# Requesting the last modulation section's weight chunks one at a time into two slots

## The chip, the cores and the metric

The kernel runs on one core of a Trainium2 chip. The metric is the device time of one execution in microseconds, as a median over runs. The core has a matrix engine (PE, with PEld for its weight loads), a vector engine (DVE), a scalar engine (ACT), a general engine (POOL), and SP, which only issues transfers. Each engine takes its own instructions strictly in the order in which they are written; engines wait for each other through semaphores. Transfers (DMA) are carried out by 16 DMA engines, fed here by two main queues: SP's requests (q1) and POOL's requests (q0).

## The reference

One conditioned decoder block on a sequence of 512 positions and a width of 1024. What matters here:

```python
mod = jax.nn.silu(c) @ w_ada + b_ada
shift1, scale1, gate1, shift2, scale2, gate2 = [m[:, None, :] for m in jnp.split(mod, 6, axis=-1)]
...
h2 = rms_norm(x, norm2_g) * (1.0 + scale2) + shift2
f_g, f_u = jnp.split(h2 @ w_ffn_in, 2, axis=-1)
x = x + gate2 * ((jax.nn.silu(f_g) * f_u) @ w_ffn_out)
```

`w_ada` is 1024 x 6144, so each of the six sections of `mod` is a vector of 1024 made from a 1024 x 1024 block of weights (4 MB). The last section, `gate2`, is needed only after the second matrix product of the feed-forward part. The first product of that part has `w_ffn_in`, 1024 x 5632 (2 x 2816 columns).

## The kernel before

**The work around the change.** After the two branches, their merge and the second norm, the kernel computes `h2 @ w_ffn_in` column group by column group, and then the last product with `w_ffn_out`. The order of all instructions is written out by hand; nothing reorders them. Every product is done as three products of rounded parts (`mm3`, lines 52 to 55), with a high part made by ACT and a low part made by DVE for each block of weights. The first pair of column groups is done in plain form; the other 20 groups are done in the loop `for q in range(-2, NQ)` (here "turn q", with NQ = 18), in which a seven-product scheme replaces eight products of half blocks. An even q handles 256 columns of the gate part `f_g` (followed by silu), an odd q the same columns of `f_u` (followed by the product with the gate part). One turn holds seven calls of `sprod`, each of twelve matmuls of 128 x 256, on four PSUM banks R[0] to R[3]; even and odd turns have different banks.

**What a turn does beside the matmuls.**

- `s_issue(q + 2)`, first thing in the turn (line 1311): SP requests the weight block of the turn after next, as two halves of 512 KB. The first half holds the blocks A11 and A21, the second A12 and A22. The buffers are a ring of three and one single buffer, so that a half can be requested when the same half of the block two turns earlier has been used up. Its last readers are DVE's L1361 (first half) and L1368 (second half), which run in turn q - 1.
- `s_prep(q + 1)` prepares the block of the next turn in four steps. ACT rounds: L1337 (A11, first half only), L1348, L1358, L1365. DVE forms sums and low parts: L1340 (A21 + A22, so both halves), L1343, L1344, L1351, L1354, L1361, L1368.
- ACT copies one bank into the next as its starting value: R[0] into R[1] (L1676), then R[1] into R[2] (L1689); two copies into `ps` (L1684, L1696). ACT's first rounding of the turn (L1337) stands ahead of the copy L1676 in its order.
- DVE adds the banks up into the result (L1701, L1704); ACT applies silu in the turns of `f_g` (L1666, L1672), DVE the product in the turns of `f_u` (L1664, L1670).
- `wstep()` (lines 1688 and 1716) lets POOL issue transfers that add up parts of `w_ffn_out` in memory, for the last product. They use POOL's queue and share the 16 engines with SP's.

**The last section.** `mod_sec(5)` yields eight chunks. A chunk is 512 KB: two slices of 128 x 512 of `w_ada`. Each has a function that requests it (line 205, on SP) and a function that uses it: two instructions of DVE on 128 x 512, here called macs, that multiply a slice by a scalar per partition and add it to `acc` (L177, or L175 for the first of each half). Chunks 0 to 3 make the first half of the section, 4 to 7 the second. `last_mod(k)` is called at the end of turns 1 to 8, with k = q - 1, after the last sums of the turn. For an even k it makes a new tile of 128 x 2 x 1024 with one buffer (tag E6), requests the chunks k and k + 1 into its two halves, and then issues the macs of chunk k; for an odd k it only issues the macs of chunk k. A new tile under the tag can be written only when the macs of the tile before have read it. In turn 9 `last_gate` uses the same buffer for the rounded result, and in turn 10 two pairs of matmuls spread it over the partitions and add it to `gate2b`.

Of the kernel before, what the change touches and what calls it, by code (L numbers as in the profile page):

```python
# [28 lines left out]
def block_kernel(ctx: ExitStack, tc: tile.TileContext, x, positions, w_ada, b_ada, w_in,  # L29
# [12 lines left out]
    def bank(k, name="bank"):  # L42
        return psum.tile([128, 512], F32, name=name, tag=f"b{k}", bufs=1)
# [28 lines left out]
    def issue(i):  # L72
        e = stream[i]
        if e["kind"] == "m" and e["early"]:
            k = mrot[0]
            mrot[0] += 1
            raw = s2pair(k % 8, F32).rearrange("p a n -> p (a n)")
        elif e["kind"] == "m" and e["mid"]:
            raw = mid.tile([128, 1024], F32, name="mraw", tag=e["mid"], bufs=1)
        else:  # L80
            raw = base.tile([128, 1024], F32, name="raw", tag="raw", bufs=RAWB)
        e["raw"] = raw
        if e["kind"] == "m":
            e["dma"](raw)
            return
        k0, nk, n = e["kts"][0], len(e["kts"]), e["n"]
        src = e["src"][k0 * 128:(k0 + nk) * 128, :]
        e["view"] = lambda t: t[:, :nk * n].rearrange("p (j n) -> p j n", j=nk)
        v = e["view"](raw)
        o = 0  # L90
        for c0, cn in (e["c0"] if isinstance(e["c0"], tuple) else ((e["c0"], n),)):
            SY.dma_start(v[:, :, o:o + cn], src[:, c0:c0 + cn].rearrange("(j p) n -> p j n", p=128))
            o += cn
# [256 lines left out]
    def t512(name, dt=F32):  # L350
        return base.tile([128, 512], dt, name=name, tag="t512", bufs=3)
# [946 lines left out]
    def s_issue(q):  # L1298
        if q >= NQ:
            return  # L1300
        c0 = (2 + q // 2) * 256 + (DFF if q % 2 else 0)
        sraw[q] = []
        both = ffn[0].tile([128, 2, 4, 2, 128], F32, name="raw", tag="E2", bufs=1) if q == -2 else None
        for kh in range(2):
            if both is not None:
                t = both[:, kh]
            elif q % 2 and kh:
                t = ffn[0].tile([128, 4, 2, 128], F32, name="raw", tag="F0" if q > 0 else "E5", bufs=1)
            else:
                t = base.tile([128, 4, 2, 128], F32, name="raw", tag="raw", bufs=RAWB)  # L1310
            SY.dma_start(t.rearrange("p j a n -> p j (a n)"),
                         w_ffn_in[kh * 512:(kh + 1) * 512, c0:c0 + 256].rearrange("(j p) n -> p j n", p=128))
            sraw[q].append(t)
# [10 lines left out]
    def s_prep(q):  # L1324

        if q >= NQ:
            return z_first()
        ra, rb = sraw[q]
        d = sd[q] = {}
        A11, A21, A12, A22 = ra[:, :, 0], ra[:, :, 1], rb[:, :, 0], rb[:, :, 1]  # L1330

        def a0():
            if q == -1:
                saw.append(sw(1, F32R, "sa"))
            d["A"] = tuple(base.tile([128, 4, 128], F32R, name="sa", tag="acc", bufs=2) if q == -2 else
                           saw[0][:, 2 * (q % 2) + e].rearrange("p (j n) -> p j n", j=4) for e in range(2))
            A.activation(d["A"][0], A11, AF.Copy)  # L1337

        def d0a():
            V.tensor_add(A21, A21, A22)  # L1340

        def d0b():
            V.tensor_sub(d["A"][1], A11, f(d["A"][0]))  # L1343
            V.tensor_sub(A11, A21, A11)  # L1344

        def a1():
            d["B"] = s_pair(q, 0)
            A.activation(d["B"][0], rb, AF.Copy)  # L1348

        def d1a():  # L1350
            V.tensor_sub(d["B"][1], rb, f(d["B"][0]))  # L1351

        def d1b():
            V.tensor_sub(rb, rb, A11[:, :, None, :].to_broadcast([128, 4, 2, 128]))  # L1354

        def a2():
            d["C"] = s_pair(q, 1)
            A.activation(d["C"][0], ra, AF.Copy)  # L1358

        def d2():  # L1360
            V.tensor_sub(d["C"][1], ra, f(d["C"][0]))  # L1361

        def a3():
            d["D"] = s_pair(q, 2)
            A.activation(d["D"][0], rb, AF.Copy)  # L1365

        def d3():
            V.tensor_sub(d["D"][1], rb, f(d["D"][0]))  # L1368
        return [(a0, d0a, d0b), (a1, d1a, d1b), (a2, d2), (a3, d3)]
# [119 lines left out]
    def gtile(m):  # L1489
        if m not in gq:  # L1490
            n = 4 if m < 20 else 2
            t = (sw((2, 3, 0)[m // 4], F32, "gq") if m < 12 else
                 ffn[0].tile([128, n, S], F32, name="gq", tag=("E5", "E6", "F1")[(m - 12) // 4], bufs=1))
            for e in range(n):
                gq[m + e] = t[:, e]
            gz[m // 4] = t
        return gq[m]
# [34 lines left out]
    mgl = list(mg)  # L1532
    mgr = []

    def last_mod(k):
        if k % 2 == 0:
            t = ffn[0].tile([128, 2, 1024], F32, name="mraw", tag="E6", bufs=1)
            mgr[:] = [t[:, 0], t[:, 1]]
            for e in range(2):
                mgl[k + e][0](mgr[e])  # L1540
        mgl[k][1](mgr[k % 2])

    def last_gate():
        t = ffn[0].tile([128, 4, S], F32R, name="ahl", tag="E6", bufs=1)
# [91 lines left out]
    def sprod(o, wb, hb, start):  # L1636
        (wh, wl), (bh, bl) = wb, hb
        for j in range(4):
            mm3(o, (wh[:, j], wl[:, j]), (bh[:, j], bl[:, j]), start and j == 0, j == 3, skip_group_check=True)

    left = []
    for q in range(-2, NQ):
        g, u = 2 + q // 2, q % 2
        d = sd[q]
        s_issue(q + 2)
        pre = s_prep(q + 1)
        half_of = lambda t, e: tuple(v[:, :, e] for v in t)
        S2_, S1_, A12, A22, S4_, S3_ = (half_of(d[k], e) for k in "CBD" for e in range(2))
        R = [bank(k, "R")[:, :256] for k in ((4, 1, 0, 7), (5, 2, 3, 6))[q % 2]]
        ps = [ffn[0].tile([128, 256], F32, name="ps", tag="rt", bufs=2) for _ in range(2)]  # L1650
        if q == NQ - 2:
            for i in W_Z[0, 0][:2]:
                issue(i)
        t0, t1 = slice(0, 256), slice(256, 512)
        if u:
            dst = [gtile(2 * g + m) for m in range(2)]
        else:
            fs[0], fs[1] = t512("fs"), t512("fs")
            dst = fs
        cur = dict(fs)  # L1660

        def out_direct(m, p, u=u, dst=dict(enumerate([dst[0], dst[1]])), cur=cur):
            if u:
                V.tensor_mul(dst[m][:, t0], cur[m][:, t0], p)  # L1664
            else:
                A.activation(dst[m][:, t0], p, AF.Silu)  # L1666

        def out_late(m, u=u, dst=dict(enumerate([dst[0], dst[1]])), cur=cur):
            if u:
                V.tensor_mul(dst[m][:, t1], dst[m][:, t1], cur[m][:, t1])  # L1670
            else:
                A.activation(dst[m][:, t1], dst[m][:, t1], AF.Silu)  # L1672

        pre[0][0]()
        sprod(R[0], d["A"], HB[0, 0], True)
        A.activation(R[1], R[0], AF.Copy)  # L1676
        for fn in pre[0][1:]:
            fn()
        while left:
            left.pop(0)()  # L1680
        if q == NQ - 1:
            issue(W_Z[0, 0][2])
        sprod(R[3], S1_, TB[1], True)
        A.activation(ps[0], R[3], AF.Copy)  # L1684
        for fn in pre[1]:
            fn()
        sprod(R[1], S2_, TB[2], False)
        wstep()
        A.activation(R[2], R[1], AF.Copy)  # L1689
        pre[2][0]()  # L1690
        pre[2][1]()
        sprod(R[0], A12, HB[1, 0], False)
        if not u:
            out_direct(0, R[0])
        sprod(R[2], S3_, TB[3], False)
        A.activation(ps[1], R[2], AF.Copy)  # L1696
        pre[3][0]()
        pre[3][1]()
        if u:
            out_direct(0, R[0])  # L1700
        V.tensor_add(dst[1][:, t1], R[3], ps[1])  # L1701
        sprod(R[1], S4_, HB[1, 1], False)
        out_late(1)
        V.tensor_add(dst[0][:, t1], R[1], ps[0])  # L1704
        sprod(R[2], A22, TB[4], False)
        out_late(0)
        left.append(lambda fn=out_direct, p=R[2]: fn(1, p))
        if 1 <= q <= 8:
            last_mod(q - 1)
        if q == 9:  # L1710
            last_gate()
        if q == 10:
            for b_ in (3, 2):
                mbank[0] = b_
                sec_tasks(one=True)
        wstep()
        if q in (9, 13, NQ - 2):
            a_sum("S1", {9: 0, 13: 2}.get(q, 1))
# [208 lines left out]
```

## Time and profile before

| | us |
|---|---|
| median of 3 runs | 822.0 (821.88 to 822.13) |
| the profiled execution | 823.29 |
| its span | 821.5 |
| PE busy | 805.9 (98%) |
| DVE busy | 686.6 (84%) |
| ACT busy | 430.9 (52%) |
| POOL busy | 166.6 (20%) |

Times of single rows count from the start of the span. "Busy" of PE counts matmuls whose ends are modelled, and they overlap. In a row of the timeline the first number is the start and the second the duration; "idle before" in square brackets names what ended the engine's wait. In the view of waits a row gives who waited, for whom, the total, how often, and the longest. In the view of transfers the last number is the time from a request to its landing. In rows of stretches the granted clock of PE, the share of DMA time and GB/s stand at the end.

### The profile page before, as it was taken

To read this page: it belongs to the slowest core of one execution; us is meant where nothing else is said; L and a number is where in the kernel's file an instruction comes from. 1 tells how busy PE (TensorE), PEld (TensorE's weight loads), DVE (VectorE), ACT (ScalarE), POOL (GpSimd) and SP (SyncE) were. 2 spreads that over 40 slices of the span, in tenths; PEclk is the share of its full clock that TensorE was granted. 3 is DMA by queue.
4 is the path that set the end of the run, shared out by engine and by line. 5 is a ranking of instruction groups with operands and counts; after the bars stand their busy time and mean duration, and the time that the engine had idled before them with its cause. 6 is when DMAs were issued, how large, how long until landed. Compare 5 with 4: busy or idle time off the path is not lost.

```text
span 821.5 us, 12945 instructions
## 1 busy us (share of the span) xinstructions
PE 805.9 (98%) x4903; PEld 719.6 (88%) x4903; DVE 686.6 (84%) x1175; ACT 430.9 (52%) x772; POOL 166.6 (20%) x186
## 2 busy tenths in 40 slices
PE   7999999999999999999999999999999999999996
PEld 6789889988888888988888899999999999888875
DVE  7989798898899648888697879889999888898686
ACT  6674445322332226665635587555555655666554
POOL 3060031363344411000010010323121322000001
PEclk9999999999999999999999999999999999999999
DMA  9974352332346563037692603989997977556763
GB/s 294 301 222 111 111 180 78 104 102 79 106 150 198 166 200 102 28 104 247 195 254 48 205 27 103 227 236 250 255 280 196 247 182 207 172 190 201 219 175 134
DMA packets 108463, 141.35 MB, mean 172 GB/s; under 512 B 6689, under 2 KB 77089, under 8 KB 108209
## 3 DMA queue, kind: packets, MB, share of 16 engines
q1 hardware_dynamic: 97296, 110.41, 43.4%
q0 software_dynamic: 10384, 29.17, 15.0%
q10 hardware_dynamic: 720, 0.95, 0.3%
q8 instruction: 38, 0.62, 0.3%
q14 instruction: 25, 0.20, 0.1%
HBM read 138.15 MB, written 25.17 MB: 199 GB/s over the span
## 4 chain that ended last, share of the span: by engine, by line
PE 79%; DMA 7%; DVE 7%; ACT 4%; issue 1%; SPq 1%; POOL 0%; POOLq 0%; ACTq 0%; DVEq 0%
PE R L53 8%; PE R L54 8%; PE R L55 8%; PE pb L53 6%; PE pb L54 6%; PE pb L55 6%; PE pfo L53 4%; PE pfo L55 4%; PE pfo L54 4%; DMA mraw<-in_w_ada_dram 3%; PE pav L54 2%; PE pav L53 2%; PE pav L55 2%; DMA s<-in_w_ada_dram 2%; DMA oraw<-in_w_out_dram 2%; PE pgb L53 2%
## 5 line engine op out<-in xcount | busy, mean ns | idle before, releaser
L112 ACT ACTIVATE hi<-raw 128x1024 fp32r<-128x1024 f32 (+2 forms) x108 | 109.3, 1013 | 105.6 <-PE pfo L55 22.0
L116 DVE TENSOR_TENSOR lo<-raw,hi 128x1024 fp32r<-128x1024 f32 (+2 forms) x72 | 83.5, 1163 | 24.3 <-ACT hi L112 23.9
L116 POOL TENSOR_TENSOR lo<-raw,hi 128x1024 fp32r<-128x1024 f32 x29 | 73.4, 2533 | 128.1 <-ACT hi L112 122.4
L53 PE MATMUL pb<-h,hi 128*128 128x512 f32 (+1 forms) x192 | 74.5, 388 | 0.0
L55 PE MATMUL pb<-h,lo 128*128 128x512 f32 (+1 forms) x192 | 73.9, 385 | 0.0
L54 PE MATMUL pb<-h,hi 128*128 128x512 f32 (+1 forms) x192 | 73.9, 385 | 0.0
L53 PE MATMUL pfo<-hi,za 128*128 128x512 f32 (+1 forms) x144 | 55.9, 388 | 0.3 <-ACT ps L1779 0.3
L55 PE MATMUL pfo<-hi,za 128*128 128x512 f32 (+1 forms) x144 | 55.8, 388 | 0.0
L54 PE MATMUL pfo<-lo,za 128*128 128x512 f32 (+1 forms) x144 | 55.8, 388 | 0.0
L177 DVE SCALAR_TENSOR_TENSOR acc<-mraw,cols,acc 128x512 f32<-128x512 f32 x49 | 39.5, 807 | 18.5 <-DMA mraw<-in_w_ada_dram 17.5
L53 PE MATMUL R<-tb,sx 128*128 128x256 f32 x160 | 45.3, 283 | 0.3 <-ACT R L1689 0.3
L54 PE MATMUL R<-tb,sx 128*128 128x256 f32 x160 | 45.1, 282 | 0.0
L322 POOL COPY sm<-sm 128x1 f32<-128x1 f32 x36 | 26.0, 723 | 93.7 <-ACT sm L321 93.7
L55 PE MATMUL R<-tb,sx 128*128 128x256 f32 x160 | 45.0, 281 | 0.0
L55 PE MATMUL R<-tb,lo 128*128 128x256 f32 x160 | 44.8, 280 | 0.0
L53 PE MATMUL R<-tb,hi 128*128 128x256 f32 x160 | 44.8, 280 | 0.0
L54 PE MATMUL R<-tb,hi 128*128 128x256 f32 x160 | 44.6, 279 | 0.0
L55 PEld LDWEIGHTS pb<-h,lo 128*128 128x128 f32 x192 | 36.0, 188 | 7.3
L54 PEld LDWEIGHTS pb<-h,hi 128*128 128x128 f32 x192 | 36.0, 188 | 6.9
L53 PEld LDWEIGHTS pb<-h,hi 128*128 128x128 f32 x192 | 36.0, 188 | 6.8
L302 POOL DMA_DIRECT2D wsum<-in_w_ffn_out_dram x24 | 21.2, 888 | 73.1 <-DMA wsum<-wsum 45.2
L54 PE MATMUL pav<-lo,h 128*128 128x256 f32 x128 | 35.8, 279 | 0.0
(387 smaller groups left out, 2656.2 us busy)
## 6 DMA issues: line engine op xcount, KB each, us to landing
raw<-in_w_ffn_in_dram SPq DMA_DIRECT2D x44, 512.0 KB, 5.9
raw<-in_w_in_dram SPq DMA_DIRECT2D x40, 512.0 KB, 3.9
wsum<-in_w_ffn_out_dram POOLq DMA_DIRECT2D x30, 512.0 KB, 8.2
mraw<-in_w_ada_dram SPq DMA_DIRECT2D x28, 512.0 KB, 4.0
raw<-wsum SPq DMA_DIRECT2D x20, 512.0 KB, 3.7
raw<-in_w_ffn_out_dram SPq DMA_DIRECT2D x16, 512.0 KB, 4.5
s<-in_w_ada_dram SPq DMA_DIRECT2D x30, 256.0 KB, 5.5
wsum<-wsum POOLq DMA_DIRECT2D x10, 512.0 KB, 5.6
```

The lines of the kernel that those rows point to most:

```text
L53: T.matmul(o, wh, rh, start=start, stop=False, **kw)
L54: T.matmul(o, wh, rlo, start=False, stop=False, **kw)
L55: T.matmul(o, wlo, rh, start=False, stop=stop, **kw)
L112: A.activation(hi[:, :m], e["raw"][:, :m], AF.Copy)
L116: e["lo"].tensor_sub(lo[:, :m], e["raw"][:, :m], f(hi[:, :m]))
L177: V.scalar_tensor_tensor(o, w, cs[:, j:j + 1], o, op0=OP.mult, op1=OP.add)
L302: P.dma_start(wsum[n][o], src, accum_op=OP.add)
L322: P.tensor_copy(t, t)
```

## The change

The tile with the two slots is made once, in turn 0 (the loop now calls `last_mod` from q = 0 with k = -1), and chunks 0 and 1 are requested there. From turn 1 on, `last_mod(k)` issues the macs of chunk k, and then requests chunk k + 2 into the slot that these macs have read. So there is one request in each of the turns 1 to 6, and none in turns 7 and 8. A request into a slot waits, on SP, for the macs that read it. The macs, their order and their turns are as before, and so are the number and size of the transfers.

```diff
     mgr = []
 
     def last_mod(k):
-        if k % 2 == 0:
+
+        if not mgr:
             t = ffn[0].tile([128, 2, 1024], F32, name="mraw", tag="E6", bufs=1)
             mgr[:] = [t[:, 0], t[:, 1]]
             for e in range(2):
-                mgl[k + e][0](mgr[e])
-        mgl[k][1](mgr[k % 2])
+                mgl[e][0](mgr[e])
+        if k >= 0:
+            mgl[k][1](mgr[k % 2])
+            if k + 2 < len(mgl):
+                mgl[k + 2][0](mgr[k % 2])
...
         out_late(0)
         left.append(lambda fn=out_direct, p=R[2]: fn(1, p))
-        if 1 <= q <= 8:
+        if 0 <= q <= 8:
             last_mod(q - 1)
         if q == 9:
             last_gate()
```

## The prediction

> **What bounds the kernel now.** I read the engine shares first, then who waited for whom on PE, then the stretches around the change, and last the single rows of SP, DVE and ACT in turns 1 to 7 of the loop.
>
> ```profile
> PE 805.9 (98%) x4903; PEld 719.6 (88%) x4903; DVE 686.6 (84%) x1175; ACT 430.9 (52%) x772; POOL 166.6 (20%) x186
> ```
>
> PE is busy for 98% of the span, so a change to transfers or to DVE can gain only what PE waits for them. In the stage from 485 to 705 us the list of waits on PE has a single entry:
>
> ```profile
> PE R L53 <- ACT R L1689: 0.3, 1, 0.3
> ```
>
> By stretches of two turns (first column the stretch, second its length, then PE busy and matmuls):
>
> ```profile
> 545.46:565.38 19.92, 19.92 (x170) 19.92 (x169) 18.73 (x27) 11.37 (x23) 5.94 (x8) 1.00 0.85 216
> 565.38:585.33 19.95, 19.95 (x170) 19.95 (x169) 18.98 (x27) 11.44 (x23) 3.67 (x5) 1.00 0.97 279
> 585.33:605.46 20.13, 20.13 (x170) 19.97 (x170) 18.72 (x27) 11.32 (x23) 6.00 (x9) 1.00 0.86 249
> ```
>
> Two turns take about 19.93 us and PE is busy in all of it. The third pair is longer by 0.2 us, and that is the wait above. DVE stands at 18.73, 18.98 and 18.72 us of these pairs, so it has about one microsecond to spare in each. DMA is at 0.85 to 0.97 of its time: transfers are dense here, and a request that goes out late will also land late.
>
> Next the rows of DVE that matter: ends of the macs (L175, L177), first use of a fresh block (L1340 needs both halves of the block), and idle time in brackets.
>
> ```profile
> 546.96 0.75 DVE L177 SCALAR_TENSOR_TENSOR acc<-mraw,cols,acc 128x512 f32<-128x512 f32 x1
> ...
> 555.30 1.53 DVE L177 SCALAR_TENSOR_TENSOR acc<-mraw,cols,acc 128x512 f32<-128x512 f32 x2
> 556.75 0.69 DVE L1340 TENSOR_TENSOR raw<-raw 128x512 f32<-128x512 f32 x1
> ...
> 559.09 1.23 DVE L1351 TENSOR_TENSOR lo<-raw,hi 128x1024 fp32r<-128x1024 f32 x1 [0.33 <-ACT hi L1348]
> ...
> 563.30 1.23 DVE L1368 TENSOR_TENSOR lo<-raw,hi 128x1024 fp32r<-128x1024 f32 x1 [0.58 <-ACT hi L1365]
> ...
> 566.73 1.54 DVE L177 SCALAR_TENSOR_TENSOR acc<-mraw,cols,acc 128x512 f32<-128x512 f32 x2 [0.28 <-DMA mraw<-in_w_ada_dram]
> 568.18 0.69 DVE L1340 TENSOR_TENSOR raw<-raw 128x512 f32<-128x512 f32 x1
> ...
> 577.30 0.69 DVE L1340 TENSOR_TENSOR raw<-raw 128x512 f32<-128x512 f32 x1
> ...
> 583.25 1.23 DVE L1368 TENSOR_TENSOR lo<-raw,hi 128x1024 fp32r<-128x1024 f32 x1 [0.41 <-ACT hi L1365]
> ...
> 587.12 0.49 DVE L175 TENSOR_SCALAR acc<-mraw,cols 128x512 f32<-128x512 f32 x1 [0.72 <-DMA mraw<-in_w_ada_dram]
> ...
> 597.43 0.68 DVE L1340 TENSOR_TENSOR raw<-raw 128x512 f32<-128x512 f32 x1
> ```
>
> The macs of an odd turn end at 547.71 (turn 1), 568.27 (turn 3) and, with 0.49 for L175 and 0.75 for L177, about 588.39 (turn 5). DVE waited for chunks only twice, 0.28 and 0.72 us, and this is all that the change can take from DVE.
>
> **The change part by part.**
>
> *Added and removed.* The same eight requests of 512 KB, the same sixteen macs, one tile of the same size. Nothing is computed or moved more often, so this part costs nothing.
>
> *What goes.* The two waits, 1.0 us of DVE. In turn 7 they reach PE, through DVE's late sums and ACT's copy of R[1] (L1676):
>
> ```profile
> 555.74 0.62 ACT L1337 ACTIVATE sa<-raw 128x512 fp32r<-128x512 f32 x1
> 556.26 0.36 ACT L1676 ACTIVATE R<-R 128x256 f32<-128x256 f32 x1
> ...
> 566.23 0.37 ACT L1676 ACTIVATE R<-R 128x256 f32<-128x256 f32 x1 [2.35 <-PE R L55]
> ...
> 576.39 0.61 ACT L1337 ACTIVATE sa<-raw 128x512 fp32r<-128x512 f32 x1
> 576.91 0.36 ACT L1676 ACTIVATE R<-R 128x256 f32<-128x256 f32 x1
> ...
> 596.52 0.61 ACT L1337 ACTIVATE sa<-raw 128x512 fp32r<-128x512 f32 x1
> 597.04 0.36 ACT L1676 ACTIVATE R<-R 128x256 f32<-128x256 f32 x1
> ```
> ```profile
> 597.46 0.39 PE L53 MATMUL R<-tb,sx 128*128 128x256 f32 x1
> ```
>
> The copy ends at 597.40, PE's third product starts at 597.46 with its matmul at 0.39 us. Gain: the 0.3 us of the wait, no more, since PE waits for nothing else. One pair length earlier each, PE wanted that copy at 597.34 - 19.95 = 577.4 and 557.5 (597.34 is 0.12 before the late start); it was there at 577.27 and 556.62. So ACT's margin is about 0.85 us in turn 3, 0.1 in turn 5 and nothing in turn 7.
>
> *What moves.* The chunks 0 and 1 are asked for a turn earlier, in turn 0, where no slot has to come free; ten microseconds more for them cost nothing. The chunks 2 to 7 are asked for one per turn, in turns 1 to 6, and each request must wait on SP until the macs of the chunk two before it, the last DVE work of that turn, have read the slot. SP takes its requests in order. Queued behind the waiting one is the weight block of turn q+3 (L1311), which before the change did not wait for the macs. The first and the last odd turn, as requested now:
>
> ```profile
> 542.82 0.37 SPq L1311 DMA_DIRECT2D raw<-in_w_ffn_in_dram  x1
> 544.63 0.37 SPq L1311 DMA_DIRECT2D raw<-in_w_ffn_in_dram  x1
> ...
> 582.88 0.37 SPq L1311 DMA_DIRECT2D raw<-in_w_ffn_in_dram  x1
> 584.51 0.37 SPq L1311 DMA_DIRECT2D raw<-in_w_ffn_in_dram  x1
> ```
>
> After the change the chunk goes out at 547.7 and the two halves of the block behind it, at some 0.45 us per request, at 548.15 and 548.6: 5.3 and 4.0 us later than now. In turn 5 they go out at 588.85 and 589.3, later by 6.0 and 4.8. In turn 3 they would go out at 568.7 and 569.15.
>
> *The price of that delay.* From request to need, the second half has 556.75 - 548.6 = 8.15 us in the first of these rounds, 577.30 - 569.15 = 8.15 in the second, and 597.43 - 589.3 = 8.1 in the third. The first half is needed by ACT's L1337, ahead of the R[1] copy on the same engine: with the margins above it has 555.74 + 0.85 - 548.15 = 8.4, then 576.39 + 0.1 - 568.7 = 7.8, then 596.52 - 588.85 = 7.7.
>
> No row shows three requests of this make-up. The nearest are the chunk pairs of now, which go out right behind the second half of a block: the first chunk of a pair is second in its row, like the first half of a block later, and the second is third. In order of request, time to landing in the last column:
>
> ```profile
> mraw<-in_w_ada_dram SPq DMA_DIRECT2D x1, 512.0 KB, 8.6
> mraw<-in_w_ada_dram SPq DMA_DIRECT2D x1, 512.0 KB, 9.3
> mraw<-in_w_ada_dram SPq DMA_DIRECT2D x1, 512.0 KB, 9.8
> mraw<-in_w_ada_dram SPq DMA_DIRECT2D x1, 512.0 KB, 14.5
> mraw<-in_w_ada_dram SPq DMA_DIRECT2D x1, 512.0 KB, 9.7
> mraw<-in_w_ada_dram SPq DMA_DIRECT2D x1, 512.0 KB, 10.6
> mraw<-in_w_ada_dram SPq DMA_DIRECT2D x1, 512.0 KB, 5.7
> mraw<-in_w_ada_dram SPq DMA_DIRECT2D x1, 512.0 KB, 7.1
> ...
> DMA to landing us min/median/max: 3.5/7.2/10.7
> ```
>
> The last line is the blocks' own today, in this stage. Second in the row: 8.6, 9.8, 9.7, 5.7, median 9.15. Third: 9.3, 14.5, 10.6, 7.1, median 9.95. I take the medians, because the requests stand in the same queue, in the same stage and in the same order of sizes. The bounds are 3.5 (no cost) and 14.5.
>
> *The sum.* Round 1: the first half is 9.15 - 8.4 = 0.75 late, and PE waits 0.75 in turn 3. The second half is 9.95 - 8.15 = 1.8 late for DVE, which makes up 0.33 + 0.58 + 0.28 = 1.2 from its idle time in turn 3, so its macs end 0.6 later. Round 2: 1.35 + 0.6 for the later request - 0.75 that PE is late already = 1.2, PE at 1.95. DVE: 1.8 less 0.41 and 0.72 idle in turn 5, 0.65 more, 1.25 in all. Round 3: 1.45 + 1.25 - 1.95 = 0.75, PE at 2.7. Less the 0.3 gained: +2.4 us. The blocks asked for in turns 2, 4 and 6 cost nothing by the same medians: DVE has 568.18 - 557.75 = 10.4 us against 9.95, and ACT waits 2.35 us for PE there anyway (the row at 566.23). If their landings come to 11 us, that cover is gone and each adds about 0.6.
>
> The profiled execution took 823.29 us with a span of 821.5; the median of the runs is 822.0. With +2.4 the first would be 825.7, the median 824.4, and that I forecast.
>
> **A rule weighed.** The rows first: third in its row, a 512 KB transfer landed after 7.1 to 14.5 us. The Trainium skill, "DMA: Bandwidth & Descriptors", section "Anatomy of one DMA", gives a fixed 2.0 us plus bytes at 436 GB/s; by it three requests of 512 KB would be there after some 5.6 us (an estimate from that page), inside every window above, and the change would cost nothing: 821.7. The fastest 512 KB here, 3.5 us, agrees with that rule; the rows of the pairs do not, as they share the engines with the queue that POOL feeds.
>
> **The rivals.**
>
> *Hidden after all.* A load spread evenly, one chunk per turn in place of two every other turn, lets bursts land as the blocks do now, at a median of 7.2 us. That is below each of the six windows (7.7 to 8.4), and only the 0.3 gain is left: 821.7. For it: the last pair took 5.7 and 7.1. Against it: three of four pairs took longer than the windows. Losses up to 1.6 us are counted here as well.
>
> *Starved by POOL's queue.* From 574 to 579 us two blocks and two chunks stood requested on SP, and yet:
>
> ```profile
> q0 software_dynamic: 408, 0.79, 101.7%
> q1 hardware_dynamic: 77, 0.08, 5.1%
> ```
>
> SP's queue (q1) moved 0.08 MB in 5 us, POOL's (q0) 0.79. If the burst of 568.3 to 569.15 falls into that stretch, its first half lands at about 580.5 and not at 576.5, 4 us late, and with 0.75 and 0.75 for the other two rounds and the 0.3 off this gives 827.2. Now that block is requested by 564.6 and is in before. The Trainium skill (same page, "Queues, rings and completion order") has each engine go round-robin between queues by packet; by that rule the burst would keep a share, and the forecast stands. This stretch does not show such a share.
>
> *Faster.* PE has no wait worth more than 0.3 us, so a real gain needs a quicker pace of the matmuls: 168 in two turns at 0.117 us is 19.65 us against 19.93 to 20.13. If chunk transfers in pairs were what slows them, even requests could give 0.35 us per pair, over the four and a half pairs of turns 0 to 8 some 1.6 us: 820.4. It decides only if PE's spacing follows the transfers, and the first pair and the second, with DMA at 0.85 and 0.97, differ by 0.03.
>
> *The change doing something else.* If a mac waited for both slots of the tile, each would wait for the newer request. The mac at 566.73 started when its own half was there, as the other half of that tile needed 14.5 us, so I give this nothing.
>
> **How the numbers follow.** Forecast mechanism 0.38, at 824.4 (822.5 to 826); hidden 0.37, at 821.7; starved 0.21, at 827.2; faster 0.04, at 820.4. About 0.2%, 1.64 us, can be told from no change. Of the forecast case a few in a hundred stay below that, of the starved none: slower 0.57, same 0.39, faster 0.04. The range runs from 821.4 (the gain, and as much again for the spread of 0.25 between the runs) to 828.4: one landing of 14.5 us in a third place, 6.3 late, less 1.5 of idle and margin, plus 1.6 from the two other rounds.
>
> **What would show it.** Right: on SP the chunk requests wait for DVE's L177 in turns 1 to 6, with the blocks within 1 us behind them; ACT's L1337 or DVE's L1340 wait for the raw blocks in turns 3, 5 and 7; PE waits for ACT's R in the same turns, 2 to 3 us together; the wait of L175 and L177 for chunks is gone. Wrong: L1337 and L1340 wait for no transfer, or they wait and PE does not, because DVE's margin is larger than the rows say; or landings of 7 us and less in the bursts.

## The result and the profile after

The changed kernel took 828.9 us (826.75 to 830.54, 6 runs) against 822.02 for the kernel before (821.88 to 823.71, 6 runs): a ratio of 1.0077, with a 95% interval of 1.0063 to 1.009. It is slower by 6.9 us, more than the 2.4 us that were forecast, and its median lies 0.5 us above the stated range, which ended at 828.4. (Ratios here and below leave out two single executions at a lower granted clock, 879.18 us at 0.851 of the kernel before and 989.43 us at 0.753 of a version below.) Its times lie in two groups, three near 827 and three near 830.5. The profiled execution is one of the first group, 826.75 us with a span of 825.0, which is 3.5 us above the profiled execution before; the readings below are of that one.

First the engine shares of its page, then the waits of PE, of DVE and ACT on transfers, and of SP, in the stage from 485 to 710 us (who waited, for whom, total, times, longest). Behind the edit the lines are numbered four higher: L1676 of before is L1680, and L1689 is L1693.

```profile
PE 806.8 (98%) x4903; PEld 720.5 (87%) x4903; DVE 686.8 (83%) x1175; ACT 430.8 (52%) x772; POOL 162.5 (20%) x186
```
```profile
PE R L53 <- ACT R L1680: 2.3, 4, 1.4
PE R L53 <- ACT R L1693: 1.6, 2, 1.3
...
DVE raw L1340 <- DMA raw<-in_w_ffn_in_dram: 7.7, 4, 2.7
...
ACT sa L1337 <- DMA raw<-in_w_ffn_in_dram: 4.9, 3, 3.7
ACT sx L1348 <- DMA raw<-in_w_ffn_in_dram: 3.1, 2, 2.2
...
SPq L205 <- DVE acc L177: 56.4, 6, 12.6
```

PE's waits in this stage were 0.3 us before; now they are 3.9. That these 3.6 us are almost the 3.5 us between the two spans is chance. The changed execution reached the loop 1.8 us sooner, needed 4.8 us more from the loop's first matmul to the first of the last product, and 0.5 us more from there to the end. The loop before and after:

```profile
504.88:705.81 200.93, 200.60 (x1687) 200.07 (x1685) 179.90 (x243) 117.14 (x236) 51.31 (x74) 1.00 0.83 224
...
503.10:708.81 205.71, 201.80 (x1687) 200.31 (x1686) 178.71 (x241) 115.98 (x235) 48.72 (x74) 1.00 0.82 219
```

A wait costs more than its row says. For the wait of 1.45 us in turn 5, matmuls that otherwise start 0.12 us apart started at 577.05 and 578.77, and the next one 0.23 later: 1.7 us lost in all, and the other four waits lost some 0.26 us beyond their rows in the same way. DVE and ACT wait for raw blocks, which they hardly did before, and SP stands 56 us, in six waits, before a chunk request, waiting for the macs. DVE no longer waits for a chunk, which is what the change takes away.

The rows of SP show the order, and the transfers the price: a chunk goes out when the macs are done, and the two halves of the block right behind it.

```profile
545.95 0.37 SPq L205 DMA_DIRECT2D mraw<-in_w_ada_dram  x1
546.41 0.97 SPq L1311 DMA_DIRECT2D raw<-in_w_ffn_in_dram  x2
...
566.14 0.37 SPq L205 DMA_DIRECT2D mraw<-in_w_ada_dram  x1
566.60 0.99 SPq L1311 DMA_DIRECT2D raw<-in_w_ffn_in_dram  x2
```

Time to landing of the two halves (last column) for the blocks that stand behind the chunk requests of turns 1, 2 and 3:

```profile
raw<-in_w_ffn_in_dram SPq DMA_DIRECT2D x1, 512.0 KB, 5.4
raw<-in_w_ffn_in_dram SPq DMA_DIRECT2D x1, 512.0 KB, 7.4
...
raw<-in_w_ffn_in_dram SPq DMA_DIRECT2D x1, 512.0 KB, 6.3
raw<-in_w_ffn_in_dram SPq DMA_DIRECT2D x1, 512.0 KB, 12.4
...
raw<-in_w_ffn_in_dram SPq DMA_DIRECT2D x1, 512.0 KB, 11.2
raw<-in_w_ffn_in_dram SPq DMA_DIRECT2D x1, 512.0 KB, 13.3
```

In turns 4 to 6 the six halves needed 6.5, 6.2, 5.9, 5.6, 9.0 and 9.3 us. The windows of the prediction are 7.7 to 8.4 us for the blocks of odd turns and up to 10.4 for those of even turns; most land within them, and three halves, at 11.2 to 13.3, are far outside. (The two of turn 6 cost 0.3.) Each of these blocks is needed two turns after the chunk request that it stands behind. By stretches of two turns, turns 2 and 3 and then 4 and 5, PE's loss lies where the three late halves were needed:

```profile
542.89:562.81 19.92, 19.92 (x170) 19.92 (x169) 18.72 (x27) 11.48 (x23) 6.04 (x7) 1.00 0.82 218
562.81:586.16 23.35, 20.59 (x170) 20.09 (x169) 17.93 (x26) 11.08 (x23) 3.59 (x7) 1.00 0.99 276
```

The first pair takes 19.92 us, as before. The second takes 23.35, 3.4 more; there PE waited 1.3 us in turn 4, for ACT's copy R[2] behind a rounding of the second half that landed after 12.4 us, and 1.4 us in turn 5, for the copy R[1] behind the first half that landed after 11.2 us. Turns 7, 8 and 9 add waits of 0.3, 0.3 and 0.2. The last of them is for a block whose request stands right behind no chunk; its halves needed 12.1 and 12.2 us, so long landings are not peculiar to requests behind a chunk.

### The profile page after: what moved, and what is told of

The parts are those of the page before. It is cut to its first block, busy times and chain, and to the rows that moved or that the text cites. A ratio compares the mean times of both kernels' runs of the same rounds, so it can differ in the third digit from the quotient of the medians.

```text
span 825.0 us, 12948 instructions
## 1 busy us (share of the span) xinstructions
PE 806.8 (98%) x4903; PEld 720.5 (87%) x4903; DVE 686.8 (83%) x1175; ACT 430.8 (52%) x772; POOL 162.5 (20%) x186
## 4 chain that ended last, share of the span: by engine, by line
PE 50%; DVE 17%; DMA 8%; ACT 3%; issue 1%; POOL 0%; SPq 0%; POOLq 0%; ACTq 0%; DVEq 0%
PE R L53 6%; PE R L54 6%; PE R L55 6%; DMA mraw<-in_w_ada_dram 4%; PE pfo L53 4%; PE pfo L55 4%; PE pfo L54 4%; DVE acc L177 3%; DMA raw<-in_w_ffn_in_dram 3%; DVE sco L718 2%; DVE m L714 2%; PE pb L53 2%; PE pb L55 2%; PE pb L54 2%; PE po L54 2%; PE po L53 2%
## 5 line engine op out<-in xcount | busy, mean ns | idle before, releaser
L177 DVE SCALAR_TENSOR_TENSOR acc<-mraw,cols,acc 128x512 f32<-128x512 f32 x49 | 39.7, 811 | 18.0 <-DMA mraw<-in_w_ada_dram 17.0
L322 POOL COPY sm<-sm 128x1 f32<-128x1 f32 x36 | 21.6, 600 | 132.0 <-ACT sm L321 132.0
L55 PE MATMUL pav<-hi,h 128*128 128x256 f32 x128 | 35.8, 280 | 0.0
```

The lines of the kernel that those rows point to most:

```text
L55: T.matmul(o, wlo, rh, start=False, stop=stop, **kw)
L177: V.scalar_tensor_tensor(o, w, cs[:, j:j + 1], o, op0=OP.mult, op1=OP.add)
L322: P.tensor_copy(t, t)
```

## The experiments

The theory: a request on SP that waits for the macs holds back the block behind it by 3 to 6 us, and the block then lands late. The first rival: it is not the wait but the traffic, one chunk in every turn. Later a second question: why some blocks are so late and most are not. Each comparison has its own runs of the kernel before beside it.

**The changed kernel again.** No edit.

> The changed kernel once more, beside the others on one chip. Its six times so far lie in two groups, near 827 and near 830.5 us. Both theories: one of the two, 826.7 to 830.6. By the queue theory (blocks stand on SP behind a chunk request that waits for the macs) PE waits 3 to 8 us for ACT's copies R in turns 4 to 9, and L1337 or L1340 wait for raw blocks there.

Measured: 827.68 us (825.68 to 829.68) against 821.99, ratio 1.007 (1.0046 to 1.0095). PE's waits in the profiled execution, 825.68 us, are 2.8 us, less than the 3 to 8 expected, and 2.5 of them are in turn 5. That turn took 14.25 us where turns take 9.94 to 9.98, so it lost 4.3 us by a wait of 2.5. The run with the odd turns, below, shows where the rest comes from.

**The chunk request behind the block.** The same requests, two turns ahead, into the same two slots, but each stands on SP behind the next turn's block:

```diff
             mgl[k][1](mgr[k % 2])
-            if k + 2 < len(mgl):
-                mgl[k + 2][0](mgr[k % 2])
...
         s_issue(q + 2)
+        if 2 <= q < len(mgl):
+            mgl[q][0](mgr[q % 2])
```

> Chunks are asked for one at a time into the two slots, after the same macs, but each request stands on SP behind the block of the next turn instead of ahead of it. Queue theory: the blocks go out as early as before the change, 5 us earlier than in the changed kernel, so 821.7 to 822.3, no waits of PE over 0.3 us in turns 3 to 9, and no waits of L175 and L177 for chunks. Rival (it is the spread of the traffic: a chunk in every turn, which takes bandwidth from the block and from POOL's transfers): the same transfers in the same turns, so 825 or more.

Measured: 821.72 us against 821.99, ratio 1.0002 (0.9992 to 1.0011). The whole loss is gone, and the traffic of each turn is the same. Its waits of PE (485 to 720 us) and of SP (525 to 626 us):

```profile
PE R L53 <- ACT R L1693: 0.3, 1, 0.3
...
SPq L205 <- DVE acc L177: 13.1, 6, 2.9
```

That one wait of PE is at 699.9 us, in the last turn of the loop, and is in the kernel before too. SP still waits for the macs, 13 us in place of 56, but nothing stands behind that wait which could have gone earlier. The traffic rival falls. DVE waited once for a block, 1.7 us, and PE did not notice.

**The wait alone.** The kernel before, with its pairs of chunks, and a request of 8 KB from `acc` that must wait for the macs:

```diff
+    probe = [dram.tile([128, 16], F32, name=f"probe{k}") for k in range(6)]
...
         mgl[k][1](mgr[k % 2])
+        if k < 6:
+            SY.dma_start(probe[k], acc[5, k // 4][:, :16])
```

> The kernel before, with its chunk pairs, and in turns 1 to 6 a request of 8 KB from acc to a scratch in memory at the end of the turn on SP, which waits for the turn's macs. So the wait alone is added, ahead of the next block, and no chunk is moved. Queue theory: blocks go out 4 to 6 us late as in the changed kernel; 825 to 830. Rival (spread of the traffic): the chunks come in pairs as before, so 822 to 822.5.

Measured: 829.3 us, ratio 1.0092 (1.0069 to 1.0115). So a wait on SP without a chunk ahead of the block is as dear as the change. But this run is no clean test of it: the pairs now also go out late, behind the late block, and DVE waited for them, which is a loss that the changed kernel does not have (its waits of DVE, 485 to 720 us):

```profile
DVE acc L177 <- DMA mraw<-in_w_ada_dram: 6.4, 2, 4.7
DVE acc L175 <- DMA mraw<-in_w_ada_dram: 2.6, 1, 2.6
```

PE's longest wait here, 3.1 us, is for ACT's copy into `ps`, for which it does not wait in the changed kernel. The run with the wait and chunks in good time, below, mends that.

**One chunk at a time, one turn ahead.** Two slots, no waiting request, half the lead:

```diff
-            for e in range(2):
-                mgl[e][0](mgr[e])
+        if k + 1 < len(mgl):
+            mgl[k + 1][0](mgr[(k + 1) % 2])
         if k >= 0:
             mgl[k][1](mgr[k % 2])
-            if k + 2 < len(mgl):
-                mgl[k + 2][0](mgr[k % 2])
```

> Chunks one at a time into the two slots, but each only one turn ahead: at the end of a turn the chunk of the next turn is asked for into the slot that the macs of the turn before have read, so SP hardly waits. Queue theory: 821.7 to 822.5; L175 or L177 may wait up to 1 us for a chunk. Rival (spread of the traffic): 825 or more.

Measured: 822.56 us, ratio 1.0003 (0.9993 to 1.0013), no wait of L175 or L177 for a chunk. One at a time costs nothing either.

**The wait, with chunks in good time.** The version with the chunk request behind the block, and the 8 KB request (`probe` as above) at the end of turns 1 to 6:

```diff
             mgl[k][1](mgr[k % 2])
+            if k < 6:
+                SY.dma_start(probe[k], acc[5, k // 4][:, :16])
...
         s_issue(q + 2)
         if 2 <= q < len(mgl):
             mgl[q][0](mgr[q % 2])
```

> The version with the chunk request behind the block, and with the 8 KB request from acc at the end of turns 1 to 6, so SP again holds the block back until the macs of the turn are done, but no chunk stands ahead of the block, and the chunks are not late as they were in the run with the wait alone (there DVE waited 9 us for its pairs). Queue theory with the wait as its main part: 824 to 829, PE waits 2 to 7 us for ACT's copies. If instead the 512 KB of the chunk ahead of the block are the main part: 821.7 to 823.

Measured: 825.16 us (821.13 to 827.23) against 822.07, ratio 1.0031 (1.0014 to 1.0048). The wait by itself makes the kernel slower. It costs less than the changed kernel did in its three sets of runs (1.0077, 1.007 and 1.0045), so the 512 KB of a chunk ahead of the block probably add to it; the intervals of the last set and of this run overlap, so how much is not settled.

**Odd turns and even turns.** The changed kernel's order in the odd turns alone, the order with the chunk behind in the even ones, and the reverse:

```diff
-            if k + 2 < len(mgl):
+            if k + 2 < len(mgl) and k % 2 == 0:
                 mgl[k + 2][0](mgr[k % 2])
...
         s_issue(q + 2)
+        if 2 <= q < len(mgl) and q % 2 == 1:
+            mgl[q][0](mgr[q % 2])
```

> The changed kernel's place of the request in the odd turns 1, 3, 5 (chunks 2, 4, 6 ahead of the next block), and the place behind the next block for the chunks 3, 5, 7. By the prediction's sum all of the loss comes from the odd turns: 824 to 828. If the even turns cost as much, since PE waited 1.3 us in turn 4 of the changed kernel for a block asked for after the macs of turn 2: 823 to 825.

> The other half: chunks 3, 5, 7 ahead of the next block in the even turns 2, 4, 6, and chunks 2, 4, 6 behind it. By the prediction's sum these turns cost nothing: 821.7 to 822.3. If they cost as much as the odd ones: 823 to 826.

Measured: odd turns 827.54 us, ratio 1.007 (1.0055 to 1.0085); even turns 828.57 us, ratio 1.0092 (1.0063 to 1.0121). Each half alone costs as much as both, so the loss is not a sum over rounds; the even turns cost more than either expectation had for them. PE's waits of the first, and the landings of the blocks behind the chunk requests of its turns 1, 3 and 5 (of two times, first half, second half):

```profile
PE R L53 <- ACT R L1682: 3.2, 1, 3.2
PE R L53 <- ACT R L1695: 0.3, 1, 0.3
```
```profile
raw<-in_w_ffn_in_dram SPq DMA_DIRECT2D x1, 512.0 KB, 4.8
raw<-in_w_ffn_in_dram SPq DMA_DIRECT2D x1, 512.0 KB, 6.9
...
raw<-in_w_ffn_in_dram SPq DMA_DIRECT2D x1, 512.0 KB, 11.4
raw<-in_w_ffn_in_dram SPq DMA_DIRECT2D x1, 512.0 KB, 13.5
...
raw<-in_w_ffn_in_dram SPq DMA_DIRECT2D x1, 512.0 KB, 5.0
raw<-in_w_ffn_in_dram SPq DMA_DIRECT2D x1, 512.0 KB, 6.1
```

One block of the three was late, and PE waited 3.2 us for it, in turn 5. (The wait of 0.3 is the one in the last turn of the loop.) But turn 5 took 16.07 us, 6.1 more than without a wait, and that covers the 5.5 us between the medians. Turn 5, the stretch of it right behind the wait, and turn 6:

```profile
572.95:589.02 16.07, 12.88 (x87) 12.68 (x85) 9.23 (x13) 6.74 (x14) 2.75 (x5) 0.79 0.90 257
579.15:585.07 5.92, 5.92 (x27) 5.92 (x28) 4.12 (x5) 3.00 (x5) 0.87 (x1) 0.50 1.08 325
...
589.02:598.96 9.94, 9.94 (x87) 9.94 (x85) 9.77 (x15) 4.87 (x9) 1.74 (x3) 1.00 0.78 231
```

Behind the wait the granted clock (third number from the end) was 0.50, and the matmuls started 0.21 us apart where they otherwise start 0.12 apart; over 27 of them that is some 2.6 us. In the changed kernel's second profile the clock was 0.88 over turn 5, behind the wait of 2.5 us, and 0.93 over turn 4 in the run with the wait alone, behind the one of 3.1. In the other profiled executions no wait of PE in the loop was longer than 1.8 us, and the clock stayed at 1.00 in the loop. So a long wait cost PE its own length and then a stretch at half speed.

With the even turns it was the blocks of turns 2 and 6, and the halves that landed after 12.6 and 13.4 us:

```profile
PE R L53 <- ACT R L1695: 3.5, 3, 1.8
PE R L53 <- ACT R L1682: 1.3, 3, 0.6
```

**Without POOL's transfers.** What may distinguish the late blocks is what POOL's queue does at that time. In the first two of the next runs, POOL's sums of parts of `w_ffn_out` are left out, and the last product reads blocks of `w_ffn_out` itself; the first is the kernel before, the second the changed one. The third is the changed kernel as it is, for the same chip:

```diff
             P.tensor_copy(t, t)
-            fn()
...
-                src, k0, c0 = wsum[key], 2 * c, 0
+                src, k0, c0 = w_ffn_out, KZ[0][2 * c], 0
```

> The kernel before without POOL's transfers: the sums of parts of w_ffn_out in memory are left out, and the last product reads blocks of w_ffn_out itself where it read the sums, so the output is not the reference's. This is the base for the next run. PE is the bound in that stage: 820.5 to 822.2.

> The changed kernel without POOL's transfers, as in the run before it (the sums are left out). If the block is late because SP's transfers share the 16 engines with POOL's: three requests in a row then land within 4 to 6 us, inside the windows of 7.7 to 8.4 us, and the time is that of its base within 0.5 us. If the late request alone is enough: 3 to 8 us above its base.

> The changed kernel a third time, beside the two without POOL's sums, on their chip: 825 to 831, with PE's waits for ACT's copies in turns 4 to 9.

Measured on one chip: the base 821.65 us, ratio 0.9995 (0.9986 to 1.0005); the changed kernel without the sums 821.27, ratio 0.9984 (0.9974 to 0.9994) to the kernel before and 0.4 us below its base; the changed kernel as it is 825.7 (823.2 to 829.97), ratio 1.0045 (1.0024 to 1.0066). Without POOL's transfers the change costs nothing. SP's wait and the landing times of the blocks between 540 and 612 us (least, median, most), in this run:

```profile
SPq L205 <- DVE acc L177: 54.0, 6, 12.6
...
DMA to landing us min/median/max: 3.5/5.0/7.0
```

and in the changed kernel, first as it was profiled above and then in this set of runs:

```profile
DMA to landing us min/median/max: 5.4/8.2/13.3
...
DMA to landing us min/median/max: 4.7/9.1/13.2
```

The requests go out as late in all three, with 54, 56 and 58 us of waiting on SP. But three in a row now land within 7.0 us, and the smallest window is 7.7. So two things make the loss: the request that is late by 3 to 6 us, and POOL's traffic, with which some of these late blocks land 4 to 6 us later than the latest without it. Either alone costs nothing that was measured: with the block on time (behind, one ahead) POOL's traffic is covered, and without POOL's traffic the late request is.

## Where the prediction was right, and where its sum was not

*The bound, and what could be gained.* Right. PE is busy for 98% before and after, and neither version with the blocks requested on time gained or lost over 0.1%.

*The gain.* Of the right size, but read from the wrong row. The only wait in PE's list, 0.3 us for L1689, is not in turn 7: it ends at 701.43, in the last turn of the loop, where the modulation section is long done, and it is still there in every version. So it is not what made the third pair of turns 0.2 us longer. What turn 7 lost by the late copy L1676 is a wait of the weight load of 0.2 us. The kernel before, the row of PE and the row of waits from 596 to 600 us:

```profile
701.43 0.39 PE L53 MATMUL R<-tb,sx 128*128 128x256 f32 x1 [0.33 <-ACT R L1689]
```
```profile
PEld R L53 <- ACT R L1676: 0.2, 1, 0.2
```

With the chunk behind the block neither PE nor the weight load waits between 485 and 690 us, so this 0.2 us is what the longer lead can give.

*The mechanism.* Right: the chunk request waits on SP for the macs, the block behind it goes out late, ACT and DVE wait for raw blocks, and PE waits for ACT's copies of R. Moving the request behind the next block on SP removes all of it.

*The size.* The sum came out too small. Forecast +2.4 us for the median; measured +6.9 in these runs, +5.7 and +4.0 in the two later sets (827.68 - 821.99, 825.7 - 821.75). In the profiled execution it was +3.5, of which the loop made +4.8. Two terms were too small: how late some landings are, and what PE loses by a wait. The sum counted a microsecond of waiting as one of time; the five waits of the profiled execution lost some 0.26 us each beyond their rows, and the waits of 2.5 and 3.2 us in two other runs cost 4.3 and 6.1.

*The landing times.* The medians of 9.15 and 9.95 us from the pairs of chunks were the wrong term. Of the twelve halves seven landed after 5.4 to 7.4 us, sooner than assumed, two after 9.0 and 9.3, and three after 11.2 to 13.3; these three made 2.7 of the 3.6 us of waits. With POOL silent there are none above 7.0. In the other two profiles of the changed kernel the blocks land anywhere from 4.7 to 13.2 us. PE loses only by the longest, and of these a median says nothing. The rival called starved has this mechanism, at the place it named: the block of turn 3, first half 11.2 us after its request, where the prediction gave it 7.8. It had 0.21 and 827.2 us, nearer to the measured time than the case that was forecast.

*The turns 2, 4 and 6.* "Cost nothing by the same medians" failed. The second half of the block of turn 2 needed 12.4 us against the 10.4 that DVE had, and PE lost 1.3 us in turn 4; the version with the even turns alone lost 6.5 us (828.57 - 822.07). The prediction had said what would happen if landings there came to 11 us, and gave it 0.6 per block.

*The sum over three rounds.* Failed as well: the losses are not one per round. In the run with the odd turns PE waited 3.2 us once, lost 6.1 by it, and nothing in the other two rounds.

*The starved rival's picture of the queue.* Too strong. Of its stretch from 574 to 579 us, too much was said: what stood requested on SP were two halves of one block and, from 577.4 on, the two chunks, not two blocks. In the stretch from 569 to 577 us, in which the late block of turn 3 was under way in the changed kernel, both queues moved data:

```profile
q0 software_dynamic: 521, 1.02, 72.3%
q1 hardware_dynamic: 846, 0.91, 36.7%
```

SP's queue had 0.91 of the 1.93 MB. The Trainium skill, "DMA: Bandwidth & Descriptors", section "Queues, rings and completion order", has the engines go round-robin between queues by packet; this stretch agrees with that in so far as both queues got a share, and the one quoted in the prediction (0.08 of 0.87 MB) does not. What sets the share in one and the other stays open. The estimate of some 5.6 us for three requests in a row, which the prediction worked out from the Trainium skill's same page, section "Anatomy of one DMA", rests on a fit that the page gives for transfers issued by the general engine (POOL), and not by SP. It is near what was seen with POOL silent (the third of three after 5.8 to 7.0 us) and not with POOL at work.

*The traffic rival that the experiments were to exclude, and the faster one.* Both fell: one chunk per turn cost nothing, and the pair of turns in which PE did not wait took 19.92 us in the changed kernel as before.

Not fully explained is why the times of the changed kernel lie apart by up to 7 us (823.2 to 829.97 on one chip). Its three profiles lost in different turns: 1.6 us in turn 4, 1.9 in turn 5 and some 0.5 in each of turns 7 to 9; 4.3 in turn 5 and 0.35 in turn 8; 3.6 in turn 5, 1.2 in turn 7 and 0.7 in turn 9. So which landing is late changes from one execution to the next. The phase of POOL's transfers against the late requests could do that; no run shows it. No version was shown to beat the kernel before: 821.72 with the chunk behind the block is the same within its interval.

## What to carry to other kernels

A request that must wait belongs behind every request of its queue that need not wait; here moving one request per turn behind the next block was worth 4 to 7 us, with the same transfers and slots. When a request is moved, work out what stands behind it and how long those have from request to need, and compare that with the longest landing in the stage, not with the median: here 13.3 us against 8.2. Then read the loss from the length of the turns, not from the waits alone, since a wait of 3.2 us cost 6.1. And a longer lead for data that hardly anybody waits for (1.0 us of DVE, 0.2 us of PE here) is worth little to begin with.

## What the runs showed of the hardware

Of three requests of 512 KB in a row on SP's queue, the second and the third landed after 4.9 to 7.0 us while POOL's queue was silent, and after 5.4 to 13.3 us while it was at work in the same stage. Six requests of 8 KB that had to wait for the macs, on the queue that also requests the weight blocks, were enough to make an 822 us kernel 3 us slower. After PE had waited 2.5 us or more, the granted clock was 0.5 for 3.4 us (waits of 2.5 and 3.1 us) or 6.8 us (wait of 3.2), and matmuls of 128 x 256 started 0.21 us apart in place of 0.12; after waits of up to 1.8 us no such stretch was seen.
